# A two-layer decoder trunk on one core: V's tiles with the forget gate in them, another recurrent stage, another attention list and a written-out opening

## The chip, the cores and the metric

The kernel runs on one core of a Trainium2 chip. Its time is the device time of one execution in microseconds (us); for several runs the median is given. A core has a matrix engine (TensorE, PE in the profile, with its weight loads as PEld), a vector engine (DVE), an activation engine (ACT), a general engine (POOL) and a synchronising engine (SP), which here issues nearly all DMAs. Each engine works through its own list of instructions in order and waits on semaphores for the others.

## The reference

256 tokens of 1024 features run through two layers. Each layer is a half-step SwiGLU FFN (1024 to 2816 and back), a token mixer, and a second half-step FFN, with RMSNorm before and after each. The mixer of the first layer is a recurrent block (RG-LRU), that of the second is attention with a forget gate; its keys, values and gates are computed from the stream after the first layer.

```
gx = x @ w_in                                  # 1024 -> 2 x 1344
gate, rec = gx[..., :D_RNN], gx[..., D_RNN:]
rec = causal_depthwise_conv(rec, conv_w, conv_b)      # 4 taps
r = sigmoid(blocks(rec) @ w_a + b_a)           # 16 blocks of 84 x 84
i = sigmoid(blocks(rec) @ w_x + b_x)
a = exp(-8 * r * softplus(-lam))
h[t] = a[t] * h[t-1] + sqrt(1 - a[t]**2) * (i * rec)[t]
out = (gelu(gate) * h) @ w_out                 # 1344 -> 1024

kv = rms_norm(h) @ w_kv                        # 1024 -> 2 x 1024, 16 heads of 64
c = cumsum(log_sigmoid(rms_norm(h) @ w_f + b_f))      # 16 gates
logits = q @ k.T + c[query] - c[key], causal; softmax; @ v; @ w_o
```

## The kernel before

**Matmuls.** Weights come from HBM as float32. For a product of nearly float32 accuracy each operand is split in a high part of the type float32r and the rest: `split` (L169) writes whi by ACT (the first four units by POOL) and wlo by DVE, and `mm3` (L184) adds three products, x high by w high, x high by w low, x low by w high. `mm3w` (L190) is the same with the weights as the stationary operand. Transposes go through TensorE, with an identity, into the banks tr and gt.

**Units of work.** The kernel is a list `items` of pairs (prep, work). A prep loads a piece of weights of up to 128 x 1024 into one of three buffers raw (SP's DMA) and splits it into one of ten pairs whi, wlo; a work multiplies it with one token tile (t = 0 or 1, 128 tokens each). Accumulators are four PSUM banks mm; gt and tr have two each. `proj_items` (L349) makes items of a projection, 512 columns wide and two rows of tiles deep; `row_items` (L395) those of a down projection, a row of 128 by all 1024 columns each, into two banks. With `rows`, the last rows of token tile 1 are kept and multiplied bank by bank at the end.

**Order.** TensorE's order is that of the program; the other engines' instructions are put in order by the framework's scheduler, except in the opening. `slot` (L325) does one half item (an item for one token tile) and then a `tick` (L84): what was deferred by a number of ticks becomes due, a next unit is prepared when a planner's reckoned landing time has passed (`prepare_next`, L307; unit i needs unit i - 10 done), and a queue of small vector steps is emptied by 0.8 us of cost a tick. `run` (L334) takes token tile 0 some items ahead of token tile 1. Other stages have lists written by hand: RG_ORDER (L818) and ATT_ORDER (L1045), in which 0g3 is gate item 3 for token tile 0, r2 is the recurrent unit 2, gw2 its gate weights, a0 a step of the attention of token tile 0, and 0 or 1 a half item.

**Opening (L1053 to L1072).** Warming matmuls on zeros (`keep_busy`, L122), the halves of x's token tile 0 (h), the first two weight units in two pieces each, then x's tile 1. `to_tp` (L213) transposes x, `to_x` (L220) makes xg by the gains (L228), xhi (L229) and xlo (L232). `stat` (L242) takes the sums of squares.

**Leaving an FFN.** `enter` (L247) squares both accumulator banks (L208), takes the root on POOL (L201, L203), updates h (L260) and has the transposes of the next stage's input deferred. After the first FFN (`normed`) h is normalised first (`norm`, L272; hn, L277) and transposed in `go` (L279, L284).

**Recurrent stage.** Gate columns come in three groups g of four (three) tiles of 126 columns. A group's accumulator is copied to tok (L592), later transposed (L757) and put through gelu (L759). A recurrent unit r makes two tiles of 126 features by 256 tokens (L623); `conv` (L631) applies the four taps on DVE (L647) and splits the result into ch (ACT, L649) and cl (DVE, L652). A gw unit (L658) loads its 84 x 84 blocks into a zeroed raw buffer by eight small DMAs (two for the last), splits it, and multiplies (L690) into gt; tanh gives the gates th (L694). `after_gates` (L703) scales th on DVE (L711), takes tanh (L714) and exp (L715), and `batch` (L732), for two units each, the roots (L739), the inputs (L744, L745), the scan (L749), the product with the gelu (L771) and its split yh (L773) and yl (L778). The output projection reads yh and yl, tiles 0 to 3 from batch 0, 4 to 7 from batch 1, 8 to 10 from batch 2; it runs by `run`.

**K, V and forget gate.** The second layer's input is kept a second time as zhi and zlo. V is two projections of 512 columns (L926, L940) with between them one unit for the 16 columns of the forget gate (L928 to L939), of 8 x 3 matmuls of 16 columns a token tile. `post_f` (L897) makes log f; its running sum is deferred by 9 ticks (L912).

## Time and profile before

| | |
|---|---|
| median of 3 runs | 1058.16 us (1056.62 to 1058.39) |
| the profiled execution | 1056.71 us |
| its span, first to last instruction | 1055.0 us |
| mean granted TensorE clock | 0.982 |
| instructions | 13090 |
| HBM read | 176.95 MB, 169 GB/s over the span |

The page gives busy time by engine, and the span in 40 slices of 26.4 us with the busy share in tenths. PEclk is the granted clock of TensorE in tenths. Among the views, the waits tell which engine sat idle before which line and what ended that; the busy time by stretch gives, between two times, the busy time and the number of records of each engine in brackets, then the granted clock, the share of the DMA engines and GB/s. A group line gives the line, the engine, output and inputs by their names in the program, the shape, the number of records, the busy time, the mean in ns, and the idle time before. Line numbers are those of the kernel before.

### The profile page before, as it was taken

The numbers are of one execution on the slowest core, as the hardware profiler recorded it, in microseconds if no ns is written. First come the engines' busy times: TensorE is split into PE (matmuls) and PEld (weight loads), VectorE is DVE, ScalarE is ACT, GpSimd is POOL, SyncE is SP. The second block draws the span as 40 slices with busy tenths as digits, with TensorE's granted clock in tenths as the row PEclk, the third lists the DMA queues.
The fourth block names the chain that finished last, engine by engine and source line by source line (L and its number), as shares of the span: only waits on it lengthen the run. The fifth ranks groups of instructions, "written<-read, shape, count | busy, mean of one in ns | idle before, by whom it ended". The sixth has DMA issues, their size and how long they took to land.

```text
span 1055.0 us, 13090 instructions
## 1 busy us (share of the span) xinstructions
PE 1019.9 (97%) x4870; PEld 843.2 (80%) x4870; DVE 624.0 (59%) x771; ACT 539.3 (51%) x739; POOL 48.7 (5%) x109
## 2 busy tenths in 40 slices
PE   7999999989978999999999999999999999999997
PEld 4778888779966888888878888888888888888885
DVE  4666554548997755554486455555476475555542
ACT  3555543538886644443355444444357574454431
POOL 4200000010001100000010000000010010000000
PEclk9999999989988999999999999999999999999999
DMA  5776655536245676655446666655563156766541
GB/s 185 236 221 196 182 188 189 160 88 161 70 158 161 203 213 192 183 181 195 142 160 181 178 180 180 195 182 184 190 203 113 49 161 178 200 180 189 190 140 40
DMA packets 90742, 178.86 MB, mean 170 GB/s; under 512 B 11694, under 2 KB 28150, under 8 KB 90678
## 3 DMA queue, kind: packets, MB, share of 16 engines
q1 hardware_dynamic: 90006, 177.94, 55.9%
q8 instruction: 38, 0.62, 0.2%
q14 instruction: 26, 0.21, 0.1%
q0 software_dynamic: 640, 0.07, 0.1%
q10 hardware_dynamic: 32, 0.01, 0.0%
HBM read 176.95 MB, written 1.05 MB: 169 GB/s over the span
## 4 chain that ended last, share of the span: by engine, by line
PE 83%; DVE 6%; ACT 4%; DMA 4%; issue 2%; POOL 1%; DVEq 0%; SPq 0%; POOLq 0%; ACTq 0%
PE mm L186 25%; PE mm L188 25%; PE mm L187 25%; DVE wlo L179 3%; PE tr L462 2%; DMA raw<-in_ffn_w_gate_dram 2%; ACT whi L178 1%; PE mm L997 1%; PE gt L970 1%; ACT junk L208 1%; DMA raw<-in_ffn_w_up_dram 1%; PE gt L217 1%; PE tr L883 1%; PE mm L195 1%; PE mm L193 1%
## 5 line engine op out<-in xcount | busy, mean ns | idle before, releaser
L179 DVE TENSOR_TENSOR wlo<-raw,whi 128x1024 fp32r<-128x1024 f32 (+3 forms) x338 | 408.0, 1210 | 312.8 <-ACT whi L178 307.6
L178 ACT ACTIVATE whi<-raw 128x1024 fp32r<-128x1024 f32 (+2 forms) x332 | 348.6, 1052 | 359.9 <-PE mm L188 290.9
L186 PE MATMUL mm<-whi,xhi 128*128 128x512 f32 (+2 forms) x784 | 312.3, 398 | 5.3 <-ACT xhi L229 3.3
L187 PE MATMUL mm<-wlo,xhi 128*128 128x512 f32 (+2 forms) x784 | 306.4, 391 | 1.5 <-DVE wlo L179 1.5
L188 PE MATMUL mm<-whi,xlo 128*128 128x512 f32 (+2 forms) x784 | 306.5, 391 | 0.0
L186 PEld LDWEIGHTS mm<-whi,xhi 128*128 128x128 f32 x784 | 148.6, 189 | 35.2 <-POOL whi L176 3.4
L188 PEld LDWEIGHTS mm<-whi,xlo 128*128 128x128 f32 x784 | 148.3, 189 | 31.7 <-DVE xlo L232 0.6
L187 PEld LDWEIGHTS mm<-wlo,xhi 128*128 128x128 f32 x784 | 148.7, 190 | 30.5 <-DVE wlo L179 2.1
L186 PE MATMUL mm<-whi,hhi 128*128 128x512 f32 x352 | 139.5, 396 | 0.0
L188 PE MATMUL mm<-whi,hlo 128*128 128x512 f32 x352 | 139.0, 395 | 0.0
L187 PE MATMUL mm<-wlo,hhi 128*128 128x512 f32 x352 | 138.7, 394 | 0.0
L188 PEld LDWEIGHTS mm<-whi,hlo 128*128 128x128 f32 x352 | 66.1, 188 | 15.4
L187 PEld LDWEIGHTS mm<-wlo,hhi 128*128 128x128 f32 x352 | 66.1, 188 | 15.3
L186 PEld LDWEIGHTS mm<-whi,hhi 128*128 128x128 f32 x352 | 66.1, 188 | 15.1
L456 DVE SCALAR_TENSOR_TENSOR prod<-mm,rstd,sil 128x512 f32<-128x512 f32 (+1 forms) x48 | 33.9, 705 | 37.8 <-PE mm L188 34.0
L447 ACT ACTIVATE sil<-mm,rstd 128x512 f32<-128x512 f32 (+1 forms) x48 | 31.3, 651 | 44.9 <-PE mm L188 44.9
L201 POOL TENSOR_SCALAR nv<-ss 128x1 f32<-128x1 f32 x24 | 9.4, 391 | 759.6 <-ACT junk L208 759.6
L256 DVE TENSOR_TENSOR t<-mm,gb 128x512 f32<-128x512 f32 x24 | 16.3, 688 | 31.1 <-ACT junk L208 30.8
L466 ACT ACTIVATE hhi<-tr 128x512 fp32r<-128x512 f32 (+1 forms) x48 | 26.6, 553 | 14.6 <-PE tr L462 14.5
L467 DVE TENSOR_TENSOR hlo<-tr,hhi 128x512 fp32r<-128x512 f32 (+1 forms) x48 | 30.5, 642 | 3.4 <-ACT hhi L466 1.5
L208 ACT ACTIVATE junk<-mm 128x512 bf16<-128x512 f32 x24 | 14.2, 592 | 33.2 <-PE mm L188 32.8
L186 PE MATMUL mm<-whi,zhi 128*128 128x512 f32 (+1 forms) x80 | 31.0, 387 | 0.0
(178 smaller groups left out, 950.7 us busy)
## 6 DMA issues: line engine op xcount, KB each, us to landing
raw<-in_ffn_w_down_dram SPq DMA_DIRECT2D x88, 512.0 KB
raw<-in_ffn_w_up_dram SPq DMA_DIRECT2D x80, 512.0 KB
raw<-in_ffn_w_gate_dram SPq DMA_DIRECT2D x78, 512.0 KB
raw<-in_rg_w_in_dram SPq DMA_DIRECT2D x20, 504.0 KB
raw<-in_w_kv_dram SPq DMA_DIRECT2D x16, 512.0 KB
raw<-in_ffn_w_gate_dram SPq DMA_DIRECT2D x20, 256.0 KB
raw<-in_rg_w_out_dram SPq DMA_DIRECT2D x10, 504.0 KB
raw<-in_ffn_w_up_dram SPq DMA_DIRECT2D x16, 256.0 KB
```

Of the source, the lines that this page charges most:

```text
L178: nc.scalar.activation(hi[:parts, c:c + m], rawv[:, c:c + m], AF.Copy)
L179: nc.vector.tensor_tensor(lo[:parts, c:c + m], rawv[:, c:c + m], hi[:parts, c:c + m].bitcast(F32), ALU.subtract)
L186: nc.tensor.matmul(ps, xh, wh, start=first, stop=False)
L187: nc.tensor.matmul(ps, xh, wl, start=False, stop=False)
L188: nc.tensor.matmul(ps, xl, wh, start=False, stop=last)
L208: nc.scalar.activation(junk[:, :src.shape[1]], src, AF.Square, scale=f, accum_out=acc)
L256: nc.vector.tensor_tensor(t1[n], pf[n], gb[:, n * 512:(n + 1) * 512], ALU.mult)
L447: nc.scalar.activation(s[:, :nn], ps, AF.Silu, scale=rs[t][:, 0:1])
L456: nc.vector.scalar_tensor_tensor(pr[:, :nn], ps, rs[t][:, 0:1], s, ALU.mult, ALU.mult)
L462: nc.tensor.transpose(tp[:, j * P:(j + 1) * P], pr[:, j * P:(j + 1) * P], ident)
L466: nc.scalar.activation(hv, tp[:, :nn], AF.Copy)
L467: nc.vector.tensor_tensor(lv, tp[:, :nn], hv.bitcast(F32), ALU.subtract)
```

## The change

**Opening.** The order is written out: raw 0 in two pieces ahead of x's tile 0, raw 1, x's tile 1, raw 2, and raw 3 once raw 0 is split. ACT splits units 0, 2 and 3, POOL unit 1. Items 0 and 1 do their x-low products last. Twelve and four warming matmuls take the place of eight and five. Items 0 to 3 are done for both token tiles before `run` starts, and no unit is prepared by the planner until then.

**Leaving an FFN.** All down projections but the last layer's last FFN keep two rows instead of one, for token tile 0 as well; so does the output projection of the recurrent stage and of the attention. After the first FFN `norm` comes at once instead of after a tick, with squares in two halves, and `go` after five ticks instead of two. The first `run` has lag_out = 8.

**Recurrent stage.** The gate weights are no longer items: each has a buffer gy of its own, is loaded at items 20, 26, 32, 38, 44 and 50 of the first FFN, and is used unsplit, in one plain float32 matmul a block on the unsplit conv output. ch and cl go. The scaling before tanh and exp goes into the activations' scale and bias, tile by tile. gelu is taken on the accumulator, in place of the copy to tok; those of (g, t) = (0, 1) and (2, 0) wait for (1, 1) and (2, 1). A batch's tt is one tile, with one root; the gates' transposes come after the scans, and the product reads them from PSUM. The lists change, and the output projection has its own list OUT_ORDER.

**V.** Three tiles of 344, 340 and 340 columns, the first with the 16 columns of the forget gate beside it, in items of two rows of tiles each; the running sum is deferred by 15 ticks.

**Attention.** ATT_ORDER has one more half item of token tile 1 ahead of the third a0, and the last a0 later.

The diff, cut to its core:

```diff
         purse[0] = min(purse[0] + SHARE, SHARE)
-        prepare_next()
+        if state["p"] >= OPEN:
+            prepare_next()
...
-            if loading[0] < FIRST:
+            if pool:
                 nc.gpsimd.tensor_scalar(hi[:parts, c:c + m], rawv[:, c:c + m], 1.0, 0.0, ALU.mult, ALU.add)
             else:
                 nc.scalar.activation(hi[:parts, c:c + m], rawv[:, c:c + m], AF.Copy)
...
         def norm():
-            stat(t)
+            ss = new_ss()
+            for n in range(2):
+                square_sum(h[t][:, n * 512:(n + 1) * 512], ss[:, n:n + 1])
+            rs[t] = rstd_of(ss, 2)
...
-            defer(2, go)
+            defer(5, go)
         if normed:
-            defer(1, norm)
+            norm()
...
+                if i < 2:
+                    for lo in (False, True):
+                        for j in range(kn):
+                            xh, xl = get_x(t, k0 + j)
+                            for w_ in ([u.hi] if lo else [u.hi, u.lo]):
+                                nc.tensor.matmul(ps, xl if lo else xh, w_[:, j * nn:(j + 1) * nn],
+                                                 start=k0 + j == 0 and not lo and w_ is u.hi, stop=False)
+                    return
...
-    def row_items(w, widths, get_x, post, rows=1):
+    def row_items(w, widths, get_x, post, rows=2):
...
-                if t == 1 and k >= nk - rows:
-                    kept.append((k, u))
+                m = rows if t == 1 else min(rows, 2)
+                if k >= nk - m:
+                    kept[t].append((k, u))
...
-                tok = pools["r"].tile([P, 4 * RT], F32, tag="tok", name=nm("tok"), bufs=4)
-                nc.scalar.activation(tok[:, :nn], ps, AF.Copy)
-                toks[(g, t)] = tok
+                if (g, t) not in ((0, 1), (2, 0)):
+                    for gg, tt_ in {(1, 1): [(0, 1)], (2, 1): [(2, 0)]}.get((g, t), []) + [(g, t)]:
+                        n = GCOLS[gg][1]
+                        tok = toks[(gg, tt_)] = pools["r"].tile([P, 4 * RT], F32, tag="tok", name=nm("tok"), bufs=4)
+                        nc.scalar.activation(tok[:, :n], gacc[(gg, tt_)][:, :n], AF.Gelu_apprx_tanh)
...
-            nc.scalar.activation(ch[:w, j, :], xc[:w, j, :], AF.Copy)
-
-        def low():
-            nc.vector.tensor_tensor(cl[:w, :m, :], xc[:w, :m, :], ch[:w, :m, :].bitcast(F32), ALU.subtract)
...
-            raw = new_raw()
-            v = raw[:w, :2 * m * n]
+            v = box["w"] = rw.tile([P, 1024], F32, tag="gy", name=nm("gw"), bufs=6)[:w, :2 * m * n]
             nc.gpsimd.memset(v, 0.0)
...
-                        mm3w(ps[:w, j * S:(j + 1) * S], u.hi[:, o:o + w], u.lo[:, o:o + w], ch[:w, k, :], cl[:w, k, :],
-                             k == 0, k == m - 1)
+                        nc.tensor.matmul(ps[:w, j * S:(j + 1) * S], wv[:, o:o + w], xc[:w, k, :],
+                                         start=k == 0, stop=k == m - 1)
...
+        ahead(20 + 6 * p, prep)
+        gw[p] = work
...
-            for j, i in enumerate(tl):
-                nc.vector.tensor_scalar(th[p][0][:w, j, :], th[p][0][:w, j, :], sp2[:w, i:i + 1], sp2[:w, i:i + 1],
-                                        ALU.mult, ALU.add)
-            tt[p] = pools["r"].tile([RT, 2, S], F32, tag="tt", name=nm("tt"), bufs=6)
-            nc.scalar.activation(tt[p][:w, :m, :], z, AF.Tanh)
-            nc.scalar.activation(z, z, AF.Exp, scale=-2.0)
+            for (dst, f, c) in ((t_, AF.Tanh, sp2), (th[p][0], AF.Exp, sp4)):
+                for j, i in enumerate(tl):
+                    nc.scalar.activation(dst[:w, j, :], th[p][0][:w, j, :], f, bias=c[:w, i:i + 1], scale=c[:w, i:i + 1])
...
+                tp = tps[t][:w, a * P:b * P].rearrange("p (a b) -> p a b", a=b - a)
+                nc.vector.tensor_tensor(y[:w, a:b, :], tp, tt[g][:w, a:b, t * P:(t + 1) * P], ALU.mult)
+                nc.scalar.activation(yy[g][0][:w, t, a:b, :], y[:w, a:b, :], AF.Copy)
...
-    RG_ORDER = ("0g0 0g1 0g2 0g3 0g4 0g5 0g6 0g7 r0 1g0 1g1 1g2 1g3 r1 gw0 1g4 1g5 r2 gw1 1g6 1g7 r3 gw2 "
-                "0g8 0g9 0g10 r4 gw3 1g8 r5 gw4 1g9 1g10 gw5").split()
+    RG_ORDER = ("0g0 0g1 0g2 0g3 0g4 0g5 0g6 0g7 r0 1g0 1g1 1g2 r1 gw0 1g3 1g4 r2 gw1 1g5 1g6 r3 gw2 1g7 "
+                "0g8 0g9 0g10 r4 gw3 r5 1g8 1g9 gw4 1g10 gw5").split()
+    OUT_ORDER = [0] * 8 + [1] * 4 + [0] * 3 + [1] * 7
...
-            defer(9, lambda: running(t))
+            defer(15, lambda: running(t))
...
-    proj_items(A["w_kv"], D, 512, z_x, post_v(0))
...
-    items.append((prep_f, work_f))
-    proj_items(A["w_kv"], D + 512, 512, z_x, post_v(1))
+    VCOLS = [(0, 344), (344, 340), (684, 340)]
+    def v_items(c0, n, extra):
...
+                nc.sync.dma_start(v[:, :, :n], A["w_kv"][rows, D + c0:D + c0 + n].rearrange("(k p) n -> p k n", p=P))
+                if extra:
+                    nc.sync.dma_start(v[:, :, n:], A["w_fgate"][rows, :].rearrange("(k p) n -> p k n", p=P))
...
+    for i, (c0, n) in enumerate(VCOLS):
+        v_items(c0, n, NH if i == 0 else 0)
...
-    ATT_ORDER = ("0 0 0 0 0 0 0 0 a0 1 a0 1 1 a0 1 a0 1 a0 1 a0 1 a0 a1 1 a0 a1 "
-                 "0 a1 0 a1 0 a1 0 a1 0 a1 0 a1 0 a1 0 a1 1 a1 1 a1 1 1 1 1 1 1")
+    ATT_ORDER = ("0 0 0 0 0 0 0 0 a0 1 a0 1 1 1 a0 1 a0 1 a0 1 a0 a1 1 a0 "
+                 "0 a1 a0 a1 0 a1 0 a1 0 a1 0 a1 0 a1 0 a1 0 a1 1 a1 1 a1 1 1 1 1 1 1")
...
-    keep_busy(8)
+    raws = [first_loads[0]()]
+    load_h(0)
+    raws.append(first_loads[1]())
+    load_h(1)
+    raws.append(first_loads[2]())
...
+    keep_busy(12)
+    first_split(0)
     gains_T(grow0, 16, 0)
     tps = [to_tp(h[0], n) for n in range(2)]
-    keep_busy(5)
-    prepare_next(True)
+    keep_busy(4)
     to_x(tps, main_dest(0, 0))
-    prepare_next(True)
-    load_h(1)
+    first_split(1)
+    raws.append(first_loads[3]())
+    state["p"] = 2
     half(0, 0)
+    tps = [to_tp(h[1], n) for n in range(2)]
     half(0, 1)
-    tps = [to_tp(h[1], n) for n in range(2)]
     to_x(tps, main_dest(0, 1))
-    stat(0)
-    stat(1)
     half(1, 0)
     half(1, 1)
+    first_split(2)
+    stat(0)
+    first_split(3)
+    stat(1)
+    state["p"] = OPEN
...
+    for i in range(2, OPEN):
+        half(0, i)
+        half(1, i)
...
-    run(n_ffn1, lag_in=3)
+    run(n_ffn1, lag_in=3, lag_out=8)
```

168 lines of the change are left out of this document (84 added, 84 removed).

## The prediction

> **What bounds the kernel now.** I read the page first: which engine is full, and where it is not.
>
> ```profile
> PE 1019.9 (97%) x4870; PEld 843.2 (80%) x4870; DVE 624.0 (59%) x771; ACT 539.3 (51%) x739; POOL 48.7 (5%) x109
> ...
> PE   7999999989978999999999999999999999999997
> ...
> PEclk9999999989988999999999999999999999999999
> ```
>
> TensorE (PE) is busy 97% of the span of 1055.0 us. The digits drop in slices 1, 9, 12 and 13 and in the last; PEclk drops in 9, 12 and 13 too, so part of what counts as busy there ran slowly. The bound is TensorE's stream of matmuls; a change pays by shortening that stream, or by removing a hole or a slow stretch from it. Next come the waits of PE over the span (total, times, longest) and the busy time by stretch (length, busy, records, granted clock).
>
> ```profile
> PE mm L186 <- ACT yh L773: 6.8, 2, 4.4
> PE gt L284 <- DVE hn L277: 4.9, 2, 3.6
> PE gt L194 <- DVE cl L652: 4.4, 1, 4.4
> PE mm L186 <- ACT xhi L229: 3.3, 2, 2.3
> ...
> PE gt L217 <- DVE h L260: 1.7, 2, 1.3
> ...
> PE gt L970 <- ACT qT L884: 1.3, 1, 1.3
> ```
> ```profile
> 160.00:180.00 20.00, 20.00 (x88) 16.16 (x87) 8.58 (x7) 7.94 (x8) 0.00 (x0) 1.00 0.57 185
> ```
> ```profile
> 206.00:220.10 14.10, 10.46 (x50) 0.94 0.78 226
> 220.10:231.00 10.90, 10.90 (x51) 0.76 0.09 19
> 250.00:290.00 40.00, 38.81 (x301) 1.00 0.40 97
> 280.00:330.00 50.00, 38.28 (x197) 0.87 0.47 145
> ```
>
> An undisturbed stretch (160 to 180) has 88 records of 512 columns in 20.00 us: 0.227 us each, 0.444 ns a column. From 280 to 330, in the recurrent stage, PE is idle 11.7 us, and at clock 0.87 loses up to 6.5 more: 18.2 us, the largest loss. Around 206 to 231, where the first FFN hands over, idle is 3.6 us, the clock costs up to 0.06 x 14.1 + 0.24 x 10.9 = 3.5, and another 1.2 of L284's 4.9 lies just before: 8.3.
>
> The profiled execution took 1056.71 us, 1.7 over its span; the median shown is 1058.16. I add against the former and put 1.45 on at the end. Less than 0.2% either way is about what a measurement of this kernel can't tell from no change.
>
> **The opening.** Rows of PE, POOL, DVE and ACT in order of time, then the matmuls into mm banks:
>
> ```profile
> 1.51 3.60 PE L126 MATMUL tr<-idle 128*128 128x512 bf16 x8 [1.51 <-DVE idle L114]
> ...
> 10.51 0.77 PE L186 MATMUL mm<-whi,xhi 128*128 128x512 f32 x1 [2.33 <-ACT xhi L229]
> ```
> ```profile
> 6.29 3.29 POOL L176 TENSOR_SCALAR whi<-raw 128x512 fp32r<-128x512 f32 x4 [4.93 <-DMA raw<-in_ffn_w_gate_dram]
> 10.87 1.13 POOL L176 TENSOR_SCALAR whi<-raw 128x1024 fp32r<-128x1024 f32 x1 [1.29 <-DMA raw<-in_ffn_w_gate_dram]
> ...
> 20.55 1.05 POOL L176 TENSOR_SCALAR whi<-raw 128x1024 fp32r<-128x1024 f32 x1
> ```
> ```profile
> 6.94 2.16 DVE L179 TENSOR_TENSOR wlo<-raw,whi 128x512 fp32r<-128x512 f32 x2 [1.41 <-POOL whi L176]
> 9.02 1.28 DVE L228 TENSOR_TENSOR xg<-gt,gT 128x512 f32<-128x512 f32 x2
> ```
> ```profile
> 25.02 3.12 ACT L178 ACTIVATE whi<-raw 128x1024 fp32r<-128x1024 f32 x3
> ```
> ```profile
> 10.45:31.45 21.00, 15.60 (x48) 0.84 0.54 168
> ```
>
> The first 48 matmuls, four items for both token tiles, are worth 48 x 0.227 = 10.9 us and fill 10.45 to 31.45. They start late because the weight split (6.94 to 9.10) stands ahead of xg on DVE. Later they starve: the fourth item's whi runs on POOL at 20.55, behind the sums of squares, and the next three on ACT only at 25.02.
>
> After: raw 0 leaves first, x's tile 0 second. The bytes are the same and arrive in the same order of place, so x's halves land where raw 0's did, by about 6.2 and 6.9 (POOL's start at 6.29 and DVE's at 6.94 mark them), and raw 0 sooner. Its split is over by then, inside the warming matmuls (12 at 3.60 / 8 = 0.45 each end at 6.9). The first transposes are done at about 7.4; from xg's start to the first matmul are 1.5 us now (9.02 to 10.51): first matmul at about 8.9. The transposes of x's tile 1 stand ahead of the second half item on PE, but x is in by 9.7 (the third raw, queued behind it, was in at 10.87). In the written order DVE holds the pace: split 1, xg, xlo, split 2, split 3, about 1.2 us each against 2.7 us of matmuls per item; I walk it to 20.9 us for the 48th (8.9 + 10.9 + 0.9 of transposes + short waits). That is 10.6 earlier. Behind it the loads set the pace: three raw buffers; run's lag of 4 wants items 4 to 7 of token tile 0 at 1.4 us intervals, one split comes every 2.2, and the gate weights' DMAs now lie in this FFN (next part); I give back 2.6. **Term: -8** (bounds -3, if x's tile 1 is late, to -10.6).
>
> **Leaving the first FFN.** Both accumulators' last two rows are taken bank by bank, so bank 0 is whole 6 matmuls ahead of bank 1's end, not 3: 0.7 us sooner. The second sum of squares goes in halves, the first beside the second half of h: 0.5. The transposes are queued one slot later (defer 5 at once instead of 1 and 2): 6 x 0.227 = 1.4. So 2.6 of the wait of 3.6 goes and all of the 1.2; what the transposes delay now is r0, two slots (2.7 us) behind them, about what xg, xhi and xlo need. Of the 3.5 of clock I take a little. **Term: -4** (0, if ACT stands behind a weight that hasn't landed, to -8).
>
> **The recurrent stage.** PE first:
>
> ```profile
> 228.85:234.55 5.70, 5.70 (x50) 1.00 0.01 3
> ```
> ```profile
> L970 PE MATMUL gt<-kT,qT 66*128 66x256 f32 x32 | 8.4, 384 | 0.0
> ```
> ```profile
> 816.45 1.08 PE L970 MATMUL gt<-kT,qT 66*128 66x256 f32 x4
> ```
>
> The unit at 228.85 is 48 split matmuls of 256 columns (and two at the edges): 0.119 each. A gate block costs three of them, 0.357. After, it is one plain F32 matmul. The nearest is L970, and its count is to be read: 32 records for the 16 heads of token tile 1, so each matmul is two records. Four records last 1.08, the last with its tail of about 0.43, so a record is 0.215 and a matmul 0.43. There are 5 x 2 x 4 + 2 = 42 blocks: 42 x (0.43 - 0.357) = **+3.1 us** of PE. The Trainium skill ("FP8 and Floating Point Precision", TensorE Precision Notes) says that true FP32 takes 4 passes through the array; by that a block would cost 4 x 0.119 = 0.476 and the sum be 1.9 us higher. No run here shows a block of 126 rows in plain F32.
>
> Then the engines that PE waits for:
>
> ```profile
> 250.00:290.00 40.00, 38.81 (x301) 37.65 (x299) 37.42 (x67) 36.82 (x59) 2.12 (x3) 1.00 0.40 97
> 290.00:330.00 40.00, 29.47 (x127) 23.41 (x128) 37.84 (x68) 32.52 (x50) 0.00 (x0) 0.84 0.52 165
> ```
> ```profile
> 326.06 0.80 PE L186 MATMUL mm<-whi,yh 126*128 126x512 f32 x1 [4.41 <-ACT yh L773]
> ```
> ```profile
> L179 DVE TENSOR_TENSOR wlo<-raw,whi 126x1008 fp32r<-126x1008 f32 x5 | 6.0, 1204 | 1.6 <-ACT whi L178 1.6
> ...
> L711 DVE TENSOR_SCALAR th<-th,sp 126x256 f32<-126x256 f32 x10 | 4.2, 420 | 0.2 <-ACT th L694 0.2
> ...
> L652 DVE TENSOR_TENSOR cl<-xc,ch 126x512 fp32r<-126x512 f32 x5 | 3.4, 684 | 0.0
> ```
> ```profile
> L739 ACT ACT_TABLE_LOAD x5 | 6.4, 1283 | 0.1
> L178 ACT ACTIVATE whi<-raw 126x1008 fp32r<-126x1008 f32 x5 | 5.2, 1041 | 2.0 <-DMA raw<-in_rg_w_x_dram 2.0
> ...
> L649 ACT ACTIVATE ch<-xc 126x256 fp32r<-126x256 f32 x10 | 4.2, 417 | 1.2 <-DVE xc L647 1.2
> ```
>
> DVE (the third busy time) is at 37.42 and 37.84 of 40: it is the local bound, and cl and yh, for which PE waits, come out of its backlog. The change takes from DVE the gate weights' low parts (6.0), the affine (4.2) and cl (3.4), with the last tile's share about 14; from ACT the gate weights' high parts (5.2), ch (4.2), the separate gelu and two or three table loads of 1.28, while tanh and exp in two pieces add a little. So DVE needs about 61 us where it worked 75, and PE about 68.3 - 6.4 + 3.1 = 65: DVE stays near, but under. The last product (yh) was there at 326.06; 13 us of DVE's work less, it comes at about 313. PE stood before it from 321.7; without the two other waits (4.4 and 6.8 - 4.4) and half the clock's 6.4, with 3.1 more, and with two more half items (2.8) in front in the new order, it asks for it at about 317. Of the 18.2 I let 4 stay: 1 where 0g9's split waits for 1g7's buffer with one slot (1.4 us) of cover for 2.3 of split, 3 for the last batch's chain through two tables. **Term: -14 + 3 = -11** (+3, if the waits only change place, to -15).
>
> What moves: the six gate weights, 42 DMAs, go to items 20 to 50 of the first FFN, past SP's weight loads.
>
> ```profile
> L673 SPq DMA_DIRECT2D raw<-in_rg_w_a_dram x5: 316/340/403, 219.6 to 277.4; - x5
> ```
>
> At 0.34 to 0.39 each they hold SP 16 us, against a load of 0.37 every 2.2; PE there takes 2.7 us an item and ten split buffers cover it, so it costs nothing once these are full. Uncovered, early in the FFN, it is part of the 2.6 above.
>
> **V with the forget gate.** The forget gate's own unit, and the stretch after each:
>
> ```profile
> 542.45:545.10 2.65, 2.65 (x18) 1.00 0.90 267
> ```
> ```profile
> 546.10:549.50 3.40, 3.40 (x10) 0.51 0.07 24
> 559.30:562.05 2.75, 2.75 (x28) 1.00 0.66 199
> 563.20:566.60 3.40, 3.40 (x9) 0.50 0.59 175
> ```
>
> A token tile's 24 matmuls of 16 columns take 2.65 us, 0.11 each (16 of the 24 read whi and are in this row, with two at its edges). V now: 96 x 0.227 + 48 x 0.11 = 27.1. After: 48 triples of 360, 340 and 340 columns, 48 x 1040 x 0.444 ns = 22.2, by the 256-column row (4% over its columns) 23.0. That is -4.5. About 1 us behind each narrow unit the clock stands at 0.5 for 3.4 us with PE full: 1.7 lost, twice. It follows both units at the same distance and stands nowhere else in this stage; without the unit I expect neither: -3.4. The Trainium skill ("TensorE: Matmul & The Clock Gate", What's actually happening) has the half rate come "after ≥1 idle window (~3.4µs)"; no idle stretch of that length stands before either, so by the rule as worded they have another cause and stay, a rival below. **Term: -8** (-4 to -8). Twelve smaller items for nine cost ACT and DVE three short fixed parts, hidden behind PE.
>
> **Pairs elsewhere and the attention list.** L217's 1.7 shrinks by the 0.7 of bank 0; one more query item ahead of the third a0 puts 1.4 us over L970's 1.3. **Term: -2** (0 to -3).
>
> **Sum.** -8 - 4 - 11 - 8 - 2 = -33: 1056.7 - 33 = 1023.7, with 1.45 for the median **1025**.
>
> **The rivals.** *Waits change place* (0.22): DVE and ACT lose busy time, but the chain gates, tanh, exp, root, scan, product stays serial and PE meets it at gw4, gw5 and the last batch as before. The term is +2 instead of -11: 1038. For it: ACT was at 36.82 of 40 as well; against it: both lose a sixth. *The opening is bound by loads* (0.09): with the 42 DMAs early, -3 instead of -8: 1030. *The clock windows at 546 and 563 stay* (0.05), for a cause that the rows don't show: 1025 + 3.4 = 1028.5. *Slower* (0.06): the first two gate accumulators of token tile 1 now keep two of the four mm banks from 1g0 until gelu after 1g7, so r1, r2 and r3 share two. r3 needs r1's bank, that is DVE's taps of r1, and so on: it decides where taps come later than one unit and a gate, 5.7 + 3.4 us, behind their unit. Four such units at 9 us are 36: 1061. Against it: the gates of each unit need the same taps earlier. My forecast has 0.58.
>
> **Range and chances.** All terms at their best give about 1013; the first rival with 4 us of spread reaches 1042. I take 1012 to 1042. Faster 0.94; within 0.2% 0.01; slower 0.05, the two from the last rival.
>
> **What would show it.** Right: the 48th matmul by about 21 us; clock 1.00 through V; no L284 wait over 1.5; DVE under 85% and PE over 95% in the recurrent stage; plain gate matmuls in two records of 0.215. Wrong: PE waits for xc, th or yh of over 6 us in sum, a half-clock window in each stage as before, or items 4 to 8 waiting for raw.

## The result, and the profile after

Measured side by side, the new kernel took 1026.56 us (median of 4 runs, 1025.94 to 1027.79) and the kernel before 1057.62 (4 runs, 1056.62 to 1058.39). The ratio is 0.9708, with a 95% interval of 0.9691 to 0.9725: 31 us less, where 33 were forecast. Line numbers from here on are those of the new kernel; `mm3` is L182 to L184 there, the weight split L174 (whi) and L175 (wlo), a gate matmul L704.

From the page of the new kernel, the same lines as before:

```profile
span 1024.2 us, 12939 instructions
...
PE 1003.3 (98%) x4831; PEld 832.3 (81%) x4831; DVE 609.4 (59%) x747; ACT 537.7 (52%) x736; POOL 47.1 (5%) x104
...
PE   9989999999999999999999999999999999999997
...
PEclk9999999999999999999999999999999999999999
```

The holes in slices 1, 9, 12 and 13 have gone, and so have the slow stretches: PEclk is 9 throughout. One 8 is new, in slice 3. The waits of PE that are left (total, times, longest):

```profile
PE tr L476 <- DVE prod L470: 3.2, 2, 2.4
PE gt L213 <- DVE h L256: 2.8, 3, 1.1
PE gt L704 <- issue: 1.8, 1, 1.8
PE tr L884 <- DVE htok L873: 1.7, 1, 1.7
...
PE mm L184 <- DVE y L788: 0.7, 1, 0.7
...
PE gt L283 <- DVE hn L276: 0.3, 1, 0.3
```

The four waits that headed the list before (6.8, 4.9, 4.4 and 3.3) are down to 0.7 and 0.3 or gone. None of their size has come in their place, but L476 (0.7 before, as L462) has grown and L884 is new; what they wait for is read below.

Where the time came from is read off the start of the same matmul in both traces (us):

| matmul | before | after | earlier by |
|---|---|---|---|
| first | 10.51 | 8.89 | 1.6 |
| 48th of the split ones | 31.32 | 21.27 | 10.1 |
| 200th | 68.59 | 61.18 | 7.4 |
| first FFN's last | 210.5 | 204.1 | 6.4 |
| first recurrent unit | 228.88 | 216.61 | 12.3 |
| recurrent output projection's last | 346.08 | 320.72 | 25.4 |
| first of K and V | 534.26 | 510.42 | 23.8 |
| last of K and V | 597.11 | 567.01 | 30.1 |
| attention's output projection, last | 860.26 | 830.17 | 30.1 |
| last of all | 1048.17 | 1017.25 | 30.9 |

Each column is one traced execution, the new kernel's the fastest of its four. In the nine other traces below that share its opening the first matmul comes at 7.9 to 9.3, the 48th at 20.4 to 21.3 and the first FFN's last at 202.3 to 205.9: by that much single traces of the same work differ.

Four stretches give all of it: the first FFN 6.4 (10.1 by its 48th matmul, of which part is lost again), the way out of it 5.9, the recurrent stage 13.1, V and K 6.2. Busy time of the last three, from the first mark of a stage to its last, first in the kernel before (leaving the first FFN, recurrent stage, V and K), then in the new one (columns as above, with PEld, DVE, ACT and POOL between PE and the clock):

```profile
210.50:228.90 18.40, 14.76 (x59) 12.04 (x58) 10.35 (x14) 6.07 (x11) 3.29 (x5) 0.81 0.46 123
228.90:346.10 117.20, 105.48 (x649) 94.01 (x648) 99.79 (x167) 91.61 (x142) 6.67 (x12) 0.94 0.46 130
534.30:597.10 62.80, 61.42 (x296) 50.57 (x295) 39.86 (x77) 31.35 (x45) 4.49 (x11) 0.95 0.56 168
```
```profile
204.10:216.60 12.50, 12.25 (x58) 9.97 (x57) 10.65 (x15) 8.85 (x15) 1.73 (x4) 1.00 0.76 221
216.60:320.70 104.10, 101.56 (x606) 90.70 (x605) 87.12 (x141) 84.56 (x124) 2.97 (x7) 1.00 0.46 139
510.40:567.00 56.60, 53.70 (x296) 47.67 (x295) 40.17 (x79) 31.98 (x48) 4.58 (x11) 1.00 0.65 205
```

Read the recurrent stage as a ledger. Before, PE was idle 117.20 - 105.48 = 11.7 and lost about 0.06 x 117.2 = 7.0 to the clock. Now it is idle 2.5 and loses none: 16.2 gained. The plain float32 blocks were to cost 3.1; 16.2 - 3.1 = 13.1, and the stage is 117.2 - 104.1 = 13.1 shorter. V and K likewise: 4.5 fewer of PE, 0.05 x 62.8 = 3.1 of clock, but 1.5 more idle, 6.1 against the 6.2 seen.

### The profile page after: what moved, and what is told of

It reads as the page before. It is cut to its first block, busy times and chain, and to the rows that moved or that the text cites. A ratio compares the mean times of both kernels' runs of the same rounds, so it can differ in the third digit from the quotient of the medians.

```text
span 1024.2 us, 12939 instructions
## 1 busy us (share of the span) xinstructions
PE 1003.3 (98%) x4831; PEld 832.3 (81%) x4831; DVE 609.4 (59%) x747; ACT 537.7 (52%) x736; POOL 47.1 (5%) x104
## 4 chain that ended last, share of the span: by engine, by line
PE 80%; DMA 6%; ACT 6%; DVE 4%; issue 2%; POOL 1%; DVEq 0%; POOLq 0%; ACTq 0%
PE mm L184 24%; PE mm L182 24%; PE mm L183 24%; DMA raw<-in_ffn_w_gate_dram 2%; DVE wlo L175 2%; DMA raw<-in_ffn_w_up_dram 2%; PE tr L476 2%; ACT whi L174 2%; PE gt L983 1%; PE mm L1010 1%; ACT junk L204 1%; DMA raw<-in_w_kv_dram 1%; DMA raw<-in_rg_w_out_dram 1%; PE gt L213 1%; PE tr L884 1%
## 5 line engine op out<-in xcount | busy, mean ns | idle before, releaser
L175 DVE TENSOR_TENSOR wlo<-raw,whi 128x1024 fp32r<-128x1024 f32 (+5 forms) x334 | 401.7, 1205 | 298.6 <-ACT whi L174 296.1
L174 ACT ACTIVATE whi<-raw 128x1024 fp32r<-128x1024 f32 (+6 forms) x333 | 347.2, 1044 | 348.1 <-PE mm L184 266.3
L182 PE MATMUL mm<-whi,xhi 128*128 128x512 f32 (+2 forms) x776 | 307.7, 396 | 0.7 <-ACT whi L174 0.7
L183 PE MATMUL mm<-wlo,xhi 128*128 128x512 f32 (+2 forms) x776 | 301.4, 388 | 0.9 <-DVE wlo L175 0.8
L184 PE MATMUL mm<-whi,xlo 128*128 128x512 f32 (+2 forms) x776 | 301.7, 389 | 0.0
L184 PEld LDWEIGHTS mm<-whi,xlo 128*128 128x128 f32 x776 | 145.7, 188 | 30.4
L183 PEld LDWEIGHTS mm<-wlo,xhi 128*128 128x128 f32 x776 | 146.0, 188 | 29.8 <-DVE wlo L175 1.9
L182 PEld LDWEIGHTS mm<-whi,xhi 128*128 128x128 f32 x776 | 145.8, 188 | 29.0 <-ACT whi L174 1.1
L182 PE MATMUL mm<-whi,hhi 128*128 128x512 f32 x352 | 139.5, 396 | 0.0
L184 PE MATMUL mm<-whi,hlo 128*128 128x512 f32 x352 | 138.8, 394 | 0.0
L184 PEld LDWEIGHTS mm<-whi,hlo 128*128 128x128 f32 x352 | 66.1, 188 | 15.4
L182 PEld LDWEIGHTS mm<-whi,hhi 128*128 128x128 f32 x352 | 66.1, 188 | 14.8
L252 DVE TENSOR_TENSOR t<-mm,gb 128x512 f32<-128x512 f32 x24 | 16.2, 689 | 33.0 <-ACT junk L204 32.9
L476 PE MATMUL tr<-ident,prod 128*128 128x128 f32 x176 | 27.1, 272 | 3.2 <-DVE prod L470 3.2
```

The lines of the kernel that those rows point to most:

```text
L174: nc.scalar.activation(hi[:parts, c:c + m], rawv[:, c:c + m], AF.Copy)
L175: nc.vector.tensor_tensor(lo[:parts, c:c + m], rawv[:, c:c + m], hi[:parts, c:c + m].bitcast(F32), ALU.subtract)
L182: nc.tensor.matmul(ps, xh, wh, start=first, stop=False)
L183: nc.tensor.matmul(ps, xh, wl, start=False, stop=False)
L184: nc.tensor.matmul(ps, xl, wh, start=False, stop=last)
L252: nc.vector.tensor_tensor(t1[n], pf[n], gb[:, n * 512:(n + 1) * 512], ALU.mult)
```

## The experiments

All start from the new kernel and undo, add or move one thing. Times are medians beside runs of the kernel before; each ratio is to that kernel, so the new kernel's 0.9708 (0.9691 to 0.9725) is what to hold them against.

### V as before

Undone: V in two projections of 512 columns, the forget gate as a unit of its own between them, the running sum deferred by 9.

```diff
-    for i, (c0, n) in enumerate(VCOLS):
-        v_items(c0, n, NH if i == 0 else 0)
+    proj_items(A["w_kv"], D, 512, z_x, post_v(0))
...
+    items.append((prep_f, work_f))
+    proj_items(A["w_kv"], D + 512, 512, z_x, post_v(1))
```

> The changed kernel with V as before: two projections of 512 columns and the forget gate's own unit of 16 columns between them. Theory (narrow matmuls cost 4.5 us of PE time and make the clock drop for one window behind each narrow unit): about 1026.6 + 6 to 8 = 1033 to 1035, with a granted clock of 0.5 for 3.4 us within 2 us of each narrow unit. Rival (the windows at 546 and 563 had another cause, such as the wait for h just before): 1031, no window behind the units or a window at another place.

1032.2 us (1028.12 to 1034.83), ratio 0.9773 (0.9742 to 0.9803). The K and V stage takes 61.4 us instead of 56.6. The two narrow units and the stretch behind each, in this kernel:

```profile
517.10:519.80 2.70, 2.70 (x26) 2.68 (x25) 1.48 (x3) 1.87 (x3) 0.93 (x2) 1.00 0.86 277
519.80:526.00 6.20, 6.20 (x28) 5.05 (x28) 5.30 (x14) 2.72 (x5) 0.00 (x0) 1.00 0.17 64
532.40:535.10 2.70, 2.70 (x27) 2.70 (x25) 1.44 (x3) 0.46 (x1) 1.22 (x2) 0.99 0.66 191
535.10:538.50 3.40, 3.40 (x10) 2.72 (x11) 2.11 (x7) 1.38 (x3) 0.00 (x0) 0.50 0.48 162
```

The half-clock window is back behind the second narrow unit, with PE busy 2.70 of 2.70 before it. Behind the first it isn't: a unit of 2.7 us brings a window often, not always (two of two in the kernel before, one of two here). With one window instead of two the total lies just under the 1033 to 1035 expected.

### The old way out of the first FFN

Undone: `norm` after a tick and in one piece, `go` after two ticks, lag_out as elsewhere.

```diff
-            defer(5, go)
+            defer(2, go)
...
-            norm()
+            defer(1, norm)
...
-    run(n_ffn1, lag_in=3, lag_out=8)
+    run(n_ffn1, lag_in=3)
```

> The changed kernel with the old way out of the first FFN: one sum of squares over the whole row, one tick before it, transposes after two ticks, lag 7 at the end. Theory (the late transposes and the halves removed the wait for hn and the slow clock behind it, 5.9 us in the trace): 1031 to 1033, a wait of 2 to 4 us before the second tile's transposes and a window at half clock behind it. Rival (the earlier opening and another order of the loads removed it): 1026 to 1028, no wait over 1 us there.

1031.59 us (1030.66 to 1032.66), ratio 0.9767 (0.9745 to 0.979). From the first FFN's last matmul to the first gate matmul it takes 32.4 us (204.3 to 236.66), against 27.9 in the new kernel. Its wait for hn, and the busy time behind it:

```profile
PE gt L280 <- DVE hn L273: 4.4, 2, 3.1
```
```profile
213.50:216.90 3.40, 3.40 (x13) 2.97 (x12) 2.44 (x5) 1.26 (x2) 0.00 (x0) 0.50 0.62 190
```

The wait for hn is back at nearly its old size, and the slow window that follows the 3.1 of idle time comes with it. One edit of the order is paid twice.

### Work added to DVE, work added to ACT

Four useless passes over each unit's conv output, by the traces 15.3 us of DVE in one kernel and 14.0 us of ACT in the other (24 passes each); nothing reads them.

```diff
+            for _ in range(4):
+                nc.vector.tensor_tensor(scr[:w, :m, :], xc[:w, :m, :], xc[:w, :m, :], ALU.subtract)
```
```diff
+            for _ in range(4):
+                nc.scalar.activation(scr[:w, :m, :], xc[:w, :m, :], AF.Copy)
```

> The changed kernel with four useless DVE subtractions of 126x512 per recurrent unit, about 13 us of DVE work in the recurrent stage, on which nothing depends; it computes the same. Theory (DVE's backlog was what PE waited for, and taking 14 us from it opened the stage): waits of PE for xc, th or y come back, 6 to 12 us, and half-clock windows with them: 1033 to 1042. Rival (the lists, the early gate weights and the single buffers opened it, not DVE's load): under 1030.

> The same with four useless ACT copies of 126x512 per recurrent unit, about 12 us of ACT work. ACT is now at 38.1 of 40 us between 250 and 290, fuller than DVE. Theory (DVE is the bound of the stage): less than with DVE's load, 1029 to 1033. Rival (ACT has become the bound): as much or more than with DVE's load, 1035 to 1042.

With DVE loaded 1031.44 us (1029.07 to 1032.19), ratio 0.9765 (0.9743 to 0.9787); with ACT loaded 1034.69 (1030.03 to 1035.56), ratio 0.9791 (0.9762 to 0.982). From the first gate matmul to the end of the output projection: 88.7 us in the new kernel, 95.0 and 95.8 here. The chief waits and the stretch from 250 to 290 of each, DVE's first:

```profile
PE mm L182 <- ACT y L789: 4.5, 1, 4.5
```
```profile
250.00:290.00 40.00, 39.13 (x256) 36.35 (x255) 39.81 (x69) 36.02 (x53) 0.00 (x0) 1.00 0.32 104
```
```profile
PE gt L710 <- issue: 3.2, 1, 3.2
```
```profile
250.00:290.00 40.00, 35.40 (x231) 32.53 (x231) 35.50 (x60) 39.78 (x63) 0.00 (x0) 0.99 0.38 113
```

Either engine, loaded, fills 39.8 of 40 us and PE waits. Four to five tenths of the added work come out as time (6.3 of 15.3, 7.1 of 14.0), part of it as the slow clock that goes with the waits: 6.8 us at 0.50 with DVE's of 4.5, 3.4 us with ACT's of 3.2. Both totals lie between the ranges of theory and rival (ACT's trace is the fastest of its four runs, 4.7 us under the median). So in the new kernel neither has much to spare, and ACT no more than DVE. That DVE alone bounds the stage falls.

### run in place of OUT_ORDER

```diff
-    for t in OUT_ORDER:
-        slot(t, nxt[t])
-        nxt[t] += 1
-    state["a"], state["b"] = nxt
+    state["a"] = state["b"] = n_rg
+    run(n_wout)
```

> The changed kernel with the output projection of the recurrent stage run by the general routine instead of its own list, so that the third batch is asked for two half items (2.8 us) earlier. Theory (the third batch is there only just in time): a wait of 1 to 3 us of PE for y, 1027 to 1030. Rival (the batch is early, the list does nothing): 1026 to 1027, no wait for y over 1 us.

1031.32 us (1028.69 to 1033.77), ratio 0.9765 (0.9748 to 0.9781). The output projection lasts 39.2 us (289.1 to 328.3), against 32.7 (288.0 to 320.7). This kernel's wait and the stretch behind it:

```profile
PE mm L182 <- ACT y L783: 3.2, 1, 3.2
```
```profile
307.90:314.70 6.80, 5.93 (x14) 4.73 (x15) 1.73 (x6) 1.06 (x1) 0.00 (x0) 0.50 0.45 143
```

3.2 us of waiting for the last batch, and behind it 6.8 us at half the clock, worth 3.4: together the 6.5 that are missing. Two half items more in front of the wait remove both. The total is over the 1027 to 1030 expected, which had only the wait in it.

### The opening: the first weight's place, and the splits

In one kernel x's tile 0 leaves ahead of the first weight, in the other the sums of squares come ahead of the splits of units 2 and 3.

```diff
-    raws = [first_loads[0]()]
     load_h(0)
+    raws = [first_loads[0]()]
```
```diff
+    stat(0)
+    stat(1)
     first_split(2)
-    stat(0)
     first_split(3)
-    stat(1)
```

> The changed kernel with x's first token tile loaded ahead of the first weight, all else as it is. Theory (the gain of the opening lies in the order of the splits and sums behind it, and the first weight's place only keeps its split off the way of xg): first matmul 0.5 to 1.5 us later than 8.9, total 1027 to 1028. Rival (the place of the first weight carries the gain): first matmul at 10.5 or later, total 1029 or more.

> The changed kernel with both sums of squares ahead of the splits of units 2 and 3 on ACT, as far as that order goes in the opening of before. Theory (starving behind the sums cost most of the opening's loss): the 48th matmul 2 us or more later than 21.3, total 1028 to 1030. Rival (ten split buffers and the loads' pace absorb it): total within 0.5 us of 1026.6.

x first: 1026.69 us (1023.79 to 1029.54), ratio 0.9729 (0.9708 to 0.975). The first matmul comes at 10.16 instead of 8.89, the first FFN's last at 204.7 instead of 204.1. Late splits: 1025.45 us (1025.24 to 1026.74), ratio 0.972 (0.9705 to 0.9734). The 48th matmul comes at 23.07 instead of 21.27, the FFN's last at 204.3. Both ends lie within the 202.3 to 205.9 above, so of the 1.3 and 1.8 us lost at the start nothing shows 180 us later: something behind the opening sets the pace whatever the opening does. The totals can't be told from the new kernel's, and the 1028 to 1030 expected of the late splits did not come.

### What sets that pace: the queue, or the buffers

First the 42 small DMAs of the gate weights, taken from SP's queue to POOL's:

```diff
-                nc.sync.dma_start(v[0:84, o:o + 84], src[3 * p])
+                nc.gpsimd.dma_start(v[0:84, o:o + 84], src[3 * p])
```

> The changed kernel with the 42 gate weight loads issued by POOL's queue instead of SP's. Theory (they hold SP among the weight loads of the first FFN and cost part of the 2.6 us given back there): the 200th split matmul at 59 to 60 instead of 61.2, the first FFN's end 1 to 2 us earlier, 1024.5 to 1026. Rival (the pace is set by the three raw buffers and the splits, not by SP's issuing): the 200th within 0.5 of 61.2, 1026 to 1027.

1028.28 us (1027.75 to 1029.88), ratio 0.9744 (0.9726 to 0.9761): the 200th matmul at 61.27, the FFN's last at 203.0, as with these loads on SP. Their issue on SP is not the pace. (The edit moves them in time too: all 42 leave between 30 and 59 us, where the new kernel has sent 11 of them by its 200th matmul.) The ratio is 0.0036 over the new kernel's, some 4 us that neither side expected; in the trace 1.7 us of it is a half-clock window at 287.8, behind a wait of L704 that none follows in the new kernel, and the rest stays open.

Then a fourth buffer for raw weights while the first FFN runs. The room comes from writing prod over sil there, which was not tried alone:

```diff
     def new_raw():
+        taken[0] += 1
+        if four() and taken[0] % 4 == 0:
+            return pools["f"].tile([P, 1024], F32, tag="rawx", name=nm("raw"), bufs=1)
...
+    def four():
+        return state["p"] < n_ffn1 - 3
...
-            landed[i] = max(landed.get(i - 1, 4.0) + LOAD, pace["t"] if i < RAW else split_at[i - RAW] + LATE)
+            landed[i] = max(landed.get(i - 1, 4.0) + LOAD, pace["t"] if i < RAW + four() else split_at[i - RAW - four()] + LATE)
...
-                pr = pool_of().tile([P, 8 * HA], F32, tag="prod", name=nm("prod"), bufs=2)
+                pr = sil[t] if normed else pool_of().tile([P, 8 * HA], F32, tag="prod", name=nm("prod"), bufs=2)
```

> The new kernel, but while the first FFN runs a fourth buffer for raw weights (every fourth weight unit lands in it), and in that FFN the hidden product written over the silu tile instead of a tile of its own, which makes the room; the planner reckons with four. Theory (behind the written-out opening the pace is that of the three raw buffers, a load that can start only when an older one is split): the 200th split matmul starts at 58.5 to 60 us, against 61.2 in the new kernel, the first FFN's last matmul at 201.5 to 203 instead of 204.1, the total is 1023.5 to 1025.5. Rival (the pace is set by HBM's and the DMA engines' rate in that stretch, or by the splits on ACT and DVE): the 200th at 61 to 62, the first FFN's end at 204 to 205, the total 1026 to 1027.5.

1021.1 us (1018.71 to 1023.88), ratio 0.9671 (0.9653 to 0.9689): faster than both kernels. The 200th matmul comes at 57.71, the first FFN's last at 197.3, 6.8 us earlier than in the new kernel and more than the theory gave it. The traced run is the fastest of five, 2.4 us under their median; by the ratios the total gains 0.0037, some 4 us, and the two intervals only just part. Busy time by stretch, the new kernel from the 48th matmul to the 200th and from 60 to 75, then the same in this one:

```profile
21.27:61.18 39.91, 37.57 (x166) 29.45 (x165) 24.48 (x24) 21.52 (x24) 11.89 (x22) 1.00 0.80 243
60.00:75.00 15.00, 12.60 (x58) 10.16 (x58) 10.05 (x10) 7.48 (x9) 0.00 (x0) 1.00 0.78 235
```
```profile
20.79:57.71 36.92, 36.82 (x167) 29.54 (x165) 26.38 (x26) 22.69 (x25) 11.86 (x22) 1.00 0.83 276
60.00:75.00 15.00, 15.00 (x70) 12.41 (x69) 8.61 (x9) 7.51 (x9) 0.00 (x0) 1.00 0.77 235
```

PE's idle time there goes from 2.34 + 2.40 to 0.10 + 0, and in the first stretch the loads run at 276 GB/s instead of 243. In order of time, what ACT's weight split waits for, around the L476 wait of the new kernel and at the same place of this one:

```profile
65.92 1.06 ACT L174 ACTIVATE whi<-raw 128x1024 fp32r<-128x1024 f32 x1 [2.09 <-DMA raw<-in_ffn_w_gate_dram]
67.01 1.23 DVE L175 TENSOR_TENSOR wlo<-raw,whi 128x1024 fp32r<-128x1024 f32 x1 [1.92 <-ACT whi L174]
...
68.15 0.74 DVE L470 SCALAR_TENSOR_TENSOR prod<-mm,rstd,sil 128x512 f32<-128x512 f32 x1
...
68.95 0.65 PE L476 MATMUL tr<-ident,prod 128*128 128x128 f32 x4 [2.40 <-DVE prod L470]
```
```profile
66.38 1.06 ACT L182 ACTIVATE whi<-raw 128x1024 fp32r<-128x1024 f32 x1 [1.27 <-PE mm L192]
```

In the new kernel prod has its inputs, but stands on DVE behind a wlo, that behind a whi on ACT, and that behind a load which hasn't landed: PE, named as waiting for DVE, waits for a DMA. With a fourth buffer the split waits for PE to free a split buffer instead, as it should where PE is the bound, and the wait of L476 (L484 here) is gone. In the new kernel ACT's split waits for landing weights up to 67.3 us and for PE from 72.5 on, here for PE from 60.4 on: up to there the loads set the pace, behind it PE.

### The old attention list, and last rows not paired

```diff
-    ATT_ORDER = ("0 0 0 0 0 0 0 0 a0 1 a0 1 1 1 a0 1 a0 1 a0 1 a0 a1 1 a0 "
-                 "0 a1 a0 a1 0 a1 0 a1 0 a1 0 a1 0 a1 0 a1 0 a1 1 a1 1 a1 1 1 1 1 1 1")
+    ATT_ORDER = ("0 0 0 0 0 0 0 0 a0 1 a0 1 1 a0 1 a0 1 a0 1 a0 1 a0 a1 1 a0 a1 "
+                 "0 a1 0 a1 0 a1 0 a1 0 a1 0 a1 0 a1 0 a1 0 a1 1 a1 1 a1 1 1 1 1 1 1")
```
```diff
-    def row_items(w, widths, get_x, post, rows=2):
+    def row_items(w, widths, get_x, post, rows=1):
...
-                m = rows if t == 1 else min(rows, 2)
+                m = rows if t == 1 else 1
...
-        row_items(wd, [P] * 22, lambda t, k: (hid[t][0][:, k, :], hid[t][1][:, k, :]), post_down, 4 if last else 2)
+        row_items(wd, [P] * 22, lambda t, k: (hid[t][0][:, k, :], hid[t][1][:, k, :]), post_down, 4 if last else 1)
```

> The changed kernel with the old attention list. My forecast's reason (one more half item ahead of the third step covers the wait of 1.3 us for the queries): 1027.5 to 1028.5 with that wait back. Rival (the stage from the first logits to the last product took as long before and after in the two traces, so the list moves the wait): within 0.7 us of 1026.6.

> The changed kernel with only the last row, not the last two, of the down and output projections taken bank by bank, for token tile 1 alone, as before. Forecast's reason (bank 0 whole 0.7 us sooner shortens each handover): 1028 to 1030, waits for h and hn up by about 0.7 each. Rival (the handovers lie under other work but for the first FFN's): 1026 to 1027.5.

The old list: 1026.6 us (1023.85 to 1027.88), ratio 0.9725 (0.9709 to 0.974), with the wait of L983 back at 1.3. From the third FFN's end to the end of the attention's output projection it takes 81.4 us; the new list takes 79.2 in the new kernel, but the old one took 79.2 too, in the kernel before. By time this stays undecided. The traces favour the new list: from the first logits to the last product it takes 54.4 us in the new kernel and in every other with it but one (53.8 with unpaired rows), the old list 55.9 here and 55.3 in the kernel before. Unpaired rows (the edit still keeps the last row of token tile 0, which the kernel before did not): 1024.92 us (1024.04 to 1029.27), ratio 0.9715 (0.9691 to 0.9739), and the waits of L213 sum to 2.6 us in three, against 2.8 in three with pairs. The pairs are worth nothing that shows.

### What slows the clock

Matmuls that nothing reads, put into the stream: 24 of 16 columns, 12 of 16, 12 of 512, and 48 of 16.

```diff
+        for at, n, cols in BURSTS:
+            if t == 0 and i == at:
+                ps = trbank()
+                for b in range(n):
+                    nc.tensor.matmul(ps[:, :cols], xhi[:, b % 8, :P], units[i].hi[:, :cols], start=True, stop=True)
```

> The changed kernel with four bursts of useless matmuls, whose results nobody reads, put between half items of undisturbed FFN stretches: 24 of 16 columns (2.7 us) and 12 of 16 columns (1.3 us) in the first layer's second FFN, 12 of 512 columns (2.7 us) and 48 of 16 columns (5.3 us) in the second layer's first FFN. PE never idles in them. Theory (an array that is nearly empty counts as idle for the clock): a window of half clock behind the 48, perhaps behind the 24, none behind the 12 and none behind the wide ones; the 24 hit or miss with where the window's bounds fall, since in the last run with the old V one of two narrow units had a window. Rival (only waiting counts as idle): no window at any burst.

1042.18 us in its single run. Busy time by stretch: behind the 24, the 12, and the 12 of full width; then the 48 themselves, and what follows from 647.4 on.

```profile
358.00:365.00 7.00, 7.00 (x35) 5.79 (x35) 3.05 (x3) 3.34 (x4) 0.00 (x0) 1.00 0.50 154
...
400.60:407.00 6.40, 6.40 (x33) 5.28 (x33) 2.81 (x4) 3.29 (x4) 0.00 (x0) 1.00 0.48 138
...
603.30:610.00 6.70, 6.70 (x31) 5.57 (x30) 2.31 (x2) 2.12 (x2) 0.00 (x0) 1.00 0.37 121
643.00:648.90 5.90, 5.90 (x49) 5.90 (x47) 1.19 (x1) 0.00 (x0) 0.00 (x0) 0.87 0.51 165
647.40:654.20 6.80, 6.80 (x21) 5.74 (x22) 1.79 (x2) 1.06 (x1) 0.00 (x0) 0.50 0.00 0
```

Of the four only the 48 slow the clock, to 0.50 for 6.8 us from 647.4 on, 4.4 us into the burst, with PE busy in every moment of it. Narrow matmuls count as too little work; the two bursts of 1.2 and 2.5 us brought nothing in this one run.

Waiting slows it too, and the fourteen traces together show by what rule. In each of them the half-clock windows start whole multiples of 3.413 us apart (in the kernel before at 10.25, 27.32, 218.46 and 293.55, which is 5, 61 and 83 times 3.413 behind the first), so they lie on a grid, placed differently in each execution. What counts is PE's idle time within one step of that grid. Between the start of the program and PE's last matmul, every step with 1.9 us or more was followed by a step at half clock, and of those with 1.4 to 1.8 some were and some not; steps with less were followed by one only behind narrow matmuls or where they ran at half clock themselves. The wait of 2.4 us of L476 in the new kernel lies in two steps, 1.3 and 1.1, and slowed nothing; with late splits L704's wait of 1.5 lies in one step. First two steps of the new kernel, then two with late splits:

```profile
64.48:67.89 3.41, 2.08 (x10) 1.38 (x8) 1.49 (x2) 1.67 (x2) 0.00 (x0) 1.00 0.90 278
67.89:71.31 3.42, 2.36 (x13) 2.02 (x14) 2.92 (x5) 2.57 (x4) 0.00 (x0) 1.00 0.64 204
```
```profile
285.19:288.60 3.41, 1.88 (x12) 1.19 (x11) 3.41 (x6) 3.36 (x7) 0.00 (x0) 1.00 0.45 151
288.60:292.01 3.41, 3.41 (x9) 2.66 (x8) 3.41 (x7) 3.38 (x6) 0.00 (x0) 0.50 0.00 0
```

In the eleven kernels other than the one before and the two loaded ones, L704's wait is 1.5 to 2.45 us long. A half-clock window follows it in five of them (x first, late splits, the old list, POOL's queue, the fourth buffer) and not in the six others, the new kernel among them. Such a window costs 1.7 us that belong to no edit.

## Why the prediction was right

The total came out 2 us from the forecast, nearer than its terms: three fell short by 1.8 to 2.8 us and two gave 2.1 and 3.1 more, so that it came so near is partly luck. The signs named for it came; that on DVE's share says little, since it was 85% of the recurrent stage before and is 84% now. Of the terms (measured ones by the table above):

- **Opening, -8: -5.2.** (6.4 by the FFN's end, 1.2 of which is the wait for hn that the forecast put into the next term.) First matmul 8.9 as forecast; 48th at 21.3 for 20.9. The mis-sized part is "I give back 2.6": 4.9 were given back, 2.6 by the 200th matmul already. The cause named, three raw buffers, is what the fourth buffer bears out (with prod written over sil, which was not tried apart); the gate weights' DMAs, named beside them, had no part that showed. The split buffers are full from about 70 us on; the last that the loads cost up to there is L476's wait of 2.4 at 69, the other half of the 4.9.
- **Leaving the first FFN, -4: -7.1.** All of the wait for hn went but 0.3. "Of the 3.5 of clock I take a little" was too cautious: the slow window is the wait's own follower, went with it, and came back with it when the old order was put back. Of the parts, the pairs of rows give nothing by the unpaired kernel; the old `norm` and `go` together bring back 4.4 us of wait.
- **Recurrent stage, -11: -13.1.** 16.2 went for the 14 forecast, 2.5 idle stay for 4. DVE came down by 99.79 - 87.12 = 12.7 (14 forecast), to 84% of the stage, PE up to 98%. Two parts were wrong without cost. "Two or three table loads fewer": there are 14 in both kernels (in the new one 5 at L730, 4 at L613, 3 at L755, 2 at L708). "Tanh and exp in two pieces add a little": 12.7 us, with the last tile's, for 7.2. ACT's groups from 216 to 322 in the new kernel, then the last tile's tanh in the kernel before:

```profile
L730 ACT ACTIVATE th<-th,sp 126x256 f32<-126x256 f32 x10 | 5.8, 596 | 0.1
L730 ACT ACTIVATE tt<-th,sp 126x256 f32<-126x256 f32 x10 | 5.7, 598 | 0.0
...
L730 ACT ACTIVATE tt<-th,sp 84x256 f32<-84x256 f32 x1 | 0.6, 592 | 0.0
```
```profile
L714 ACT ACTIVATE tt<-th 84x256 f32<-84x256 f32 x1 | 0.4, 402 | 0.0
```

  A piece of 256 columns with its own scale and bias takes 0.60, a pass of 512 without took 0.63. The last tile's tanh has 256 columns in both kernels, 0.40 without them and 0.59 with: of the 0.56 that two pieces cost over one pass, about 0.38 is scale and bias, the rest the splitting. So ACT lost 7.0 us of work where I had counted on 12 or more; from 250 to 290 it is the fuller engine, 38.10 of 40 against DVE's 36.45:

```profile
250.00:290.00 40.00, 38.19 (x252) 35.45 (x251) 36.45 (x61) 38.10 (x55) 0.00 (x0) 1.00 0.36 118
```

  The one wait of 1.8 there, which the trace gives to "issue", is by the order ACT's too; with ACT loaded it grows to 3.2. ACT in order of time:

```profile
281.43 1.28 ACT L755 ACT_TABLE_LOAD   x1
282.73 1.06 ACT L755 ACTIVATE tt<-tt 126x1024 f32<-126x1024 f32 x1
283.69 1.04 ACT L174 ACTIVATE whi<-raw 126x1024 fp32r<-126x1024 f32 x1
284.75 1.28 ACT L708 ACT_TABLE_LOAD   x1
286.05 1.57 ACT L708 ACTIVATE th<-gt,hb 126x256 f32<-126x256 f32 x4
```

  The last unit's gates need one of two gt banks, both full until tanh has read them. The first two of the four tanh end at about 286.9, PE goes on at 286.99; ahead of them stand a root, a split and two table loads, 4.6 us. "DVE is the local bound" was true of the kernel before by its busy time; after the change the two are level, as the loaded kernels show. The forecast had the last batch's product there 4 us before PE asks for it (313 against 317); it came 0.7 after (L788's wait), and 3.2 after where the two half items in front are missing (the kernel with `run`). The sum held since PE's own work had become the longest.
- **The gate matmuls, +3.1.** As worked out: from the timeline at 232.01, 16 records last 3.62, of which the last one's tail is 0.40.

```profile
232.01 3.62 PE L704 MATMUL gt<-xc,gw 126*126 126x256 f32 x16
```

  3.22 / 15 = 0.215 a record and two records a matmul: 0.43 in place of 0.357. The Trainium skill ("FP8 and Floating Point Precision", TensorE Precision Notes) has true FP32 take four passes, by which 0.476 is the estimate; this trace has 3.6 times the split kind's 0.119, and the measurement decides. It doesn't speak against four passes: 0.43 for 4 x 256 columns is 0.42 ns a column, against 0.444 in the stream of 512.
- **V with the forget gate, -8: -6.2.** PE's 4.5 and the clock's 3.1 came. A new wait took 1.5 of them: K heads' transposes, L884. DVE, then PE, around it:

```profile
544.49 1.23 DVE L175 TENSOR_TENSOR wlo<-raw,whi 128x1024 fp32r<-128x1024 f32 x1 [1.21 <-ACT whi L174]
545.63 0.75 DVE L873 TENSOR_SCALAR htok<-mm,rstd 128x512 f32<-128x512 f32 x1
```
```profile
546.53 0.60 PE L884 MATMUL tr<-ident,htok 128*66 128x128 f32 x4 [1.72 <-DVE htok L873]
```

  The order is that of L476: htok behind a wlo that itself waited for its whi. In the forecast the smaller items were "hidden behind PE"; that a split in front of the one thing PE needs next can't be hidden was left out. The kernel with V as before hasn't this wait, but no kernel here moved that split alone, so the cause is read from the order.
- **The rest, -2: +0.7.** Between the output projection's last matmul and the first of K and V 1.5 us are lost, 1.1 of them a wait of L213 at 326.3 that the kernel before hasn't; the rest stays open. 0.8 come back at the end.

Of the rivals, the windows staying in V, "for a cause that the rows don't show", was half right: the cause isn't idle time, but it is the narrow matmuls, so it went with them. By the Trainium skill ("TensorE: Matmul & The Clock Gate", What's actually happening) the half rate comes after an idle window of some 3.4 us; the burst of 48 brought it with no idle time at all, and waits of 1.5 to 2.8 us brought it too, so by these runs the rule as worded is too narrow: a window need not be idle from end to end, and nearly empty matmuls don't make it a busy one. The slower rival, two mm banks held, left no wait: no row of PE waits for xc or for an mm bank in the new kernel's list.

## What to carry to other kernels

Price a hole in TensorE's stream together with the slow clock behind it: here a wait of 3 us cost up to 6.5, and an order that puts two more half items in front of it gained both. When an opening is made quicker, look at what paces the loads behind it; part of its gain was handed back to three landing buffers, and a fourth brought it back. Before two traces are compared to a microsecond or two, look for a half-clock window that only one of them has. A wait that names a vector instruction whose inputs are long there is to be followed up its queue, to the split and the load ahead of it.

## What was not expected of the hardware

- A stream of 48 matmuls of 16 columns, 5.9 us without a gap, brought 6.8 us at a clock of 0.50 in its one run; streams of 2.6 us brought 3.4 us of it three times out of five, over three kernels.
- Half-clock windows stand on a grid of 3.413 us, and PE's idle time within one step decides, not the length of a wait: waits of 1.5 (late splits, at 287.7), 1.9 (`run`, at 57.5) and 2.5 (x first, at 58.0) were followed by one, waits of 2.4 (the new kernel, at 69.0; the bursts, at 289.6) were not.
- A plain float32 matmul of 256 columns is two records of 0.215 us, 3.6 times a float32r one of 0.119.
- A scale and bias for each partition forces one activation a tile and costs 0.19 us in each: 0.40 without and 0.59 with for 84 by 256, 0.63 for 126 by 512 without.
